# Splitting the feed-forward's first weights during the last tile of the O projection

## The chip, the cores and the metric

The kernel runs on one core of one Trainium2 chip. TensorE (PE) does the matmuls, VectorE (DVE) and ScalarE (ACT) the element-wise work, GpSimd (POOL) some of it and some DMA issues, SyncE (SP) issues most DMAs. The metric is the device time of one execution in microseconds (us); the median of three runs counts.

## The reference

One layer of an encoder block on a sequence of 1024 tokens with 1024 channels, all in fp32:

```python
h = rmsnorm(x, g_mix_pre) * (1 + scale_m) + shift_m
z = h @ w_in                       # attention, pooling, convolution, gates
merged = gate0 * (br_a @ wa) + gate1 * (br_b @ wb) + gate2 * (br_c @ wc)
y = merged @ w_out                 # the O projection
x = x + gate_m * rmsnorm(y, g_mix_post)
h2 = rmsnorm(x, g_ff_pre) * (1 + scale_f) + shift_f
y2 = square(relu(h2 @ w_ff1)) @ w_ff2      # 1024 -> 4096 -> 1024
return x + gate_f * rmsnorm(y2, g_ff_post)
```

## The kernel before, in words

Every matmul operand is kept as two parts of a reduced fp32 format, hi and lo. A split is two instructions: ACT copies the value into the reduced format (hi, L693), and DVE subtracts that copy from the value (lo, L694). A product then is three matmuls for each 128 rows of the contraction: hi by hi, hi by lo, lo by hi.

The part that the change touches lies in the middle of the program, between the merge of the branches and the feed-forward.

**The O projection.** `out_tile(t)` makes one tile of 128 tokens, t = 0 to 7. For each half n of the 1024 output columns it runs 8 steps of k with 3 matmuls each (L1030 to L1032), 48 in all. Its inputs are the merged branches, eight tiles `mg`, split tile by tile into `mh` and `ml` (L997, L998); tile t+1 is split within tile t. When a half is done, ACT squares it with a running sum (L1033). When both are, comes a short chain over ACT and DVE: the reciprocal root of the sum (L232 on ACT, L233 to L239 on DVE), the normalisation, which reads the two PSUM banks (L1040), the sum with x (L1042), its squares (L1044), a second reciprocal root, and the normalised tile `yt` (L1046). The even tiles use the PSUM banks `mm`, the odd ones the two banks `s`.

**The transposes.** `h2T_pair(tp)` transposes the tiles 2tp and 2tp+1 on PE (L1055; four groups of four, in the banks `pt` and `pu`), and ACT and DVE make the feed-forward's operands of them (L1061, L1065, L1068, L1069): `B11`, `B21` from the pairs 0 and 1, `B12`, `B22` from the pairs 2 and 3. The pairs 0 and 1 stand in the program ahead of the tiles 3 and 5, pair 2 behind tile 7, pair 3 behind the first product of the feed-forward. Of the first two pairs, the values also go to DRAM (`h_d`), to be read back later (`hr`, L1183).

**The feed-forward's start.** It is a fast form of block multiplication: for each of 16 column tiles j of the first weights, `first_two(j)` makes two products of 12 matmuls each (`product`, L725 to L727), into a bank X with B11 and into the one bank Y with B21; `last_five(j)` makes five more. The first products of j = 0 to 4 (`EARLY = 5`) are made in a row; meanwhile the sums T1 to T4 of the operands are formed (L734) and split, and the sums of the weights too: `prep_s21(0)` (L704, L705) needs two weight tiles, loaded again by L699, `prep_s34(0)` (L712, L713) as well. `last_five(0)` takes all of these.

**Order.** The tile framework orders the instructions of each engine when the program is built, by their place in the program and by its own estimate of when each can run; the engines then work through their queues in that order. A pool's tiles reuse addresses of a closed pool, and no instruction on a new pool's tile stands ahead of the instructions of the pool that it replaces. `opool` holds the O projection's tiles; when it closes, `fpool` opens in its place, and the PSUM pool `fps` replaces `psum`. The operands `op` of the feed-forward are in `fpool`. `mpool`, the general pool, stays open: its tag `M` has eight buffers of 128x1024 fp32 (4 KB a partition). The eight `mg` tiles fill them; when tile 7 has been split, they are handed on: to `yt` of the tiles 6 and 7, to the weight tiles `w1r` of j = 0 to 4, and to `hr`. The names and lines below are those of the kernel before.

Of the kernel before, what the change touches and what calls it, by code (L numbers as in the profile page):

```python
# [9 lines left out]
F32R = mybir.dt.float32r  # L10
BF16 = mybir.dt.bfloat16
AF = mybir.ActivationFunctionType
# [5 lines left out]
KT = D // P  # L18
# [3 lines left out]
HALF = 512  # L22
# [31 lines left out]
def kernel(  # L54
# [18 lines left out]
    V, A, G, T = nc.vector, nc.scalar, nc.gpsimd, nc.tensor  # L73
# [5 lines left out]
    def open_pool(name, **kw):  # L79
        guards[name] = tc.tile_pool(name=name, bufs=1, reuse_waits="tile", **kw)  # L80
        return guards[name].__enter__()
# [4 lines left out]
    mpool = open_pool("mpool")  # L86
# [16 lines left out]
    def ps(tag, shape=(P, HALF)):  # L103
        if tag == "pt" and two[0]:
            two[1] ^= 1
            tag = ("pt", "pu")[two[1]]
        uid[0] += 1
        return psum.tile(list(shape), F32, tag=tag, name=f"ps_{tag}_{uid[0]}", bufs=PBUFS[tag])

    def f32(ap):  # L110
        return ap.bitcast(F32)
# [76 lines left out]
    for n in range(2):  # L188
        pcb = ps("pt")
        for i in range(4):  # L190
            k = 4 * n + i
# [35 lines left out]
    def rstd(ssq, r):  # L227


        n = ssq.shape[-1]  # L230
        u, w, q = (small.tile([P, n], F32, tag=f"r{i}", name="ru") for i in range(3))
        A.activation(u, ssq, AF.Sqrt, bias=epst, scale=0.25 / D)  # L232
        V.tensor_scalar(w, ssq, 0.25 / D, 0.25 * EPS, op0=ALU.mult, op1=ALU.add)  # L233
        V.reciprocal(q, u)
        for i in range(n):
            cs = slice(i, i + 1)
            V.scalar_tensor_tensor(out=w[:, cs], in0=w[:, cs], scalar=q[:, cs], in1=u[:, cs],
                                   op0=ALU.mult, op1=ALU.add)
        return V.reciprocal(r, w)  # L239
# [417 lines left out]
    for hd in range(NH):  # L657
        p = hd // 2
# [26 lines left out]
    def tile_of(pool, tag, bufs, shape=(P, D), dtype=F32, name=None):  # L685
        uid[0] += 1
        return pool.tile(list(shape), dtype, tag=tag, name=f"{name or tag}_{uid[0]}", bufs=bufs)
# [4 lines left out]
    def fsplit(hi, lo, src):  # L692
        i = A.activation(hi, src, AF.Copy)  # L693
        V.tensor_tensor(out=lo, in0=src, in1=f32(hi), op=ALU.subtract)  # L694
        return i

    def load_half(src):
        r = tile_of(mpool, "M", 8, name="w1r")
        nc.sync.dma_start(r, src)  # L699
        return r  # L700
# [19 lines left out]
    def product(p, o, c0, bs, start):  # L720
        for k in range(4):
            ks = slice(c0 + k * P, c0 + (k + 1) * P)
            a, b = o[:, 0, ks], o[:, 1, ks]
            r0, r1 = bs[k]
            T.matmul(p, a, r0, start=(start and k == 0), stop=False, skip_group_check=True)  # L725
            T.matmul(p, a, r1, start=False, stop=False, skip_group_check=True)  # L726
            i = T.matmul(p, b, r0, start=False, stop=(k == 3), skip_group_check=True)  # L727
        return i

    def two_parts(t):  # L730
        return t[:, 0, :], t[:, 1, :]
# [87 lines left out]
    def gate_pair(b, j, r1, o, first, hook):  # L819
# [5 lines left out]
        more_ada(n_ada)  # L825
        X = ps("mm")
        product(X, o, 0, q11, True)
        p1 = snap_of(g_sn(), X)
        Y = ps("av")
# [129 lines left out]
    for j in range(KT):  # L959
# [6 lines left out]
        for n, b in enumerate((1, 2, 0)):  # L966
            for hf in range(2):
                cs = slice(hf * HALF, (hf + 1) * HALF)
                pp = gemm_T(wts, br, KB[b], hf, BT[b][hf])
                o = m if b == 1 else tmp  # L970
# [20 lines left out]
    def split_mg(t):  # L991

        tk = slice(t * P, (t + 1) * P)
        mh = tile_of(opool, f"mh{t % 2}", 1, (P, KT, P), F32R)
        ml = tile_of(opool, f"ml{t % 2}", 1, (P, KT, P), F32R)
        for k in range(KT):
            A.activation(mh[:, k, :], mg[k][:, tk], AF.Copy)  # L997
            V.tensor_tensor(out=ml[:, k, :], in0=mg[k][:, tk], in1=f32(mh[:, k, :]), op=ALU.subtract)  # L998
        return mh, ml
# [5 lines left out]
    ssy = tile_of(opool, "ssy", 1, (P, NT, 2))  # L1005
# [7 lines left out]
    B12 = [tile_of(h2pool, "b12", 4, (P, HALF)) for _ in range(4)]  # L1013
    B22 = [tile_of(h2pool, "b22", 4, HT, F32R) for _ in range(4)]

    def out_tile(t):

        xt = tile_of(opool, "x2", 2)
        nc.sync.dma_start(xt, x[t])
        mh, ml = mhl.pop(0)  # L1020
        if t < NT - 1:
            mhl.append(split_mg(t + 1))
        pss = []

        yt = tile_of(opool, "yt", 4) if t < 6 else tile_of(mpool, "M", 8, name="yt")
        for n in range(2):
            p = ps("mm" if t % 2 == 0 else "s")
            ns = slice(n * HALF, (n + 1) * HALF)
            for k in range(KT):
                T.matmul(p, mh[:, k, :], wo[k][0][:, ns], start=(k == 0), stop=False)  # L1030
                T.matmul(p, mh[:, k, :], wo[k][1][:, ns], start=False, stop=False)
                T.matmul(p, ml[:, k, :], wo[k][0][:, ns], start=False, stop=(k == KT - 1))  # L1032
            A.activation(yt[:, ns], p, AF.Square, accum_out=ssy[:, t, n:n + 1])  # L1033
            pss.append(p)
        V.tensor_tensor(out=ssy1[:, t:t + 1], in0=ssy[:, t, 0:1], in1=ssy[:, t, 1:2], op=ALU.add)
        rstd(ssy1[:, t:t + 1], rsy[:, t:t + 1])
        for n in range(2):
            ns = slice(n * HALF, (n + 1) * HALF)
            y = yt[:, ns]
            V.scalar_tensor_tensor(out=y, in0=pss[n], scalar=rsy[:, t:t + 1], in1=gmb[:, ns],  # L1040
                                   op0=ALU.mult, op1=ALU.mult)
            V.tensor_tensor(out=xt[:, ns], in0=xt[:, ns], in1=y, op=ALU.add)  # L1042
        nc.gpsimd.dma_start(x2_d[t], xt)
        A.activation(yt, xt, AF.Square, accum_out=ss2[:, t:t + 1])  # L1044
        rstd(ss2[:, t:t + 1], rs2[:, t:t + 1])
        V.tensor_scalar(yt, xt, rs2[:, t:t + 1], None, op0=ALU.mult)  # L1046
        return yt

    def h2T_pair(tp, xs, bank, h_tile):
        for k0 in range(0, KT, 2):  # L1050
            p = bank()
            for kk in range(2):
                for i in range(2):
                    o = kk * 256 + i * P
                    T.transpose(p[:, o:o + P], xs[i][:, (k0 + kk) * P:(k0 + kk + 1) * P], ident)  # L1055
            for kk in range(2):
                k = k0 + kk
                cs = slice((tp % 2) * 256, (tp % 2 + 1) * 256)
                src = p[:, kk * 256:(kk + 1) * 256]
                if tp >= 2 and k < 4:  # L1060
                    A.activation(B12[k][:, cs], src, AF.Identity, bias=modc[:, 24 + k:25 + k], scale=af[:, k:k + 1])  # L1061
                    continue
                b = B11[k] if k < 4 else (B22 if tp >= 2 else B21)[k - 4]
                h = h_tile()[:, 0:256]
                A.activation(h, src, AF.Identity, bias=modc[:, 24 + k:25 + k], scale=af[:, k:k + 1])  # L1065
                if tp < 2:
                    nc.gpsimd.dma_start(h_d[k // 2][:, k % 2, cs], h)
                A.activation(b[:, 0, cs], h, AF.Copy)  # L1068
                V.tensor_tensor(out=b[:, 1, cs], in0=h, in1=f32(b[:, 0, cs]), op=ALU.subtract)  # L1069

    h2t = lambda: tile_of(opool, "h2t", 3, (P, 256))
    pairs = []
    for tp in range(4):
        x0 = out_tile(2 * tp)
        if 0 < tp < 3:
            h2T_pair(tp - 1, pairs[tp - 1], lambda: ps("pt"), h2t)
        pairs.append((x0, out_tile(2 * tp + 1)))
    h2T_pair(2, pairs[2], lambda: ps("pt"), h2t)

    close_pool("opool")  # L1080
    close_pool("wopool")
# [5 lines left out]
    def fbank(tag, bufs):  # L1087
        return tile_of(fps, tag, bufs, (P, HALF))
# [6 lines left out]
    def prep_a(j):  # L1095
        r = load_half(w_ff1[j])
        o = f_op()
        fsplit(o[:, 0, :], o[:, 1, :], r)
        return r, o
# [17 lines left out]
    def snap(p):  # L1117
        s_ = tile_of(fpool, "sn", 3, (P, HALF))
        A.activation(s_, p, AF.Copy)
        return s_  # L1120

    def plus(p, s_):
        V.tensor_tensor(out=s_, in0=p, in1=s_, op=ALU.add)
        return s_
# [1 line left out]
    prod_i = [None]  # L1126

    def first_two(j):
        r1, o = prep_a(j)
        X = fbank("X", 5)  # L1130
        product(X, o, 0, [two_parts(t) for t in B11], True)
        s1 = snap(X)
        Y = fbank("Y", 1)
        prod_i[0] = product(Y, o, HALF, [two_parts(t) for t in B21], True)
        c = plus(Y, s1)
        if j < EARLY:

            r = tile_of(fpool, "ur", 3, (P, HALF))
            A.activation(c, c, AF.Relu)
            A.activation(r, c, AF.Square)  # L1140
            nc.gpsimd.dma_start(u_d[0][j // 2][:, j % 2, :], r)
        else:
            relu2(0, j, c)
        return X, r1
# [220 lines left out]
    for t in range(NT):  # L1365
# [5 lines left out]
        for n, y in order:  # L1371
            ns = slice(n * HALF, (n + 1) * HALF)
# [6 lines left out]
        for n, _ in order:  # L1379
            ns = slice(n * HALF, (n + 1) * HALF)  # L1380
# [71 lines left out]
```

## Time and profile before

| | us |
|---|---|
| median of three runs | 1443.53 (1442.56 to 1444.18) |
| the profiled execution's own time | 1444.37 |
| its span in the profile | 1442.5 |
| PE busy | 1395.1 (97% of the span) |
| DVE busy | 1011.9 (70%) |
| ACT busy | 630.1 (44%) |

Times in the profile are counted from the start of the span. "Busy" is the time in which an engine executes instructions. A row of a timeline gives start, duration, engine, line, operation, what is written and read, its shape and how many alike follow each other; in brackets stands how long the engine was idle before it, and what it then waited for. The O projection runs from 713.9 to 806.9 us, the feed-forward's first products start at 815.25 us.

### The profile page before, as it was taken

To read this page: it belongs to the slowest core of one execution; us is meant where nothing else is said; L and a number is where in the kernel's file an instruction comes from. 1 tells how busy PE (TensorE), PEld (TensorE's weight loads), DVE (VectorE), ACT (ScalarE), POOL (GpSimd) and SP (SyncE) were. 2 spreads that over 40 slices of the span, in tenths; PEclk is the share of its full clock that TensorE was granted. 3 is DMA by queue.
4 is the path that set the end of the run, shared out by engine and by line. 5 is a ranking of instruction groups with operands and counts; after the bars stand their busy time and mean duration, and the time that the engine had idled before them with its cause. 6 is when DMAs were issued, how large, how long until landed. Compare 5 with 4: busy or idle time off the path is not lost.

```text
span 1442.5 us, 18454 instructions
## 1 busy us (share of the span) xinstructions
PE 1395.1 (97%) x6599; PEld 1149.4 (80%) x6599; DVE 1011.9 (70%) x1907; ACT 630.1 (44%) x1112; POOL 202.9 (14%) x313
## 2 busy tenths in 40 slices
PE   6999999999999999999999899999999999999997
PEld 5998888887877777778788678888888788888875
DVE  7653589796979866378756698555553448997587
ACT  6712466456844433342155563333332343434353
POOL 1002334333311101100012011111111000000230
PEclk9999999999999999999999999999999999999999
DMA  8411111202136765377523534333322886535333
GB/s 307 178 45 46 58 30 60 89 30 85 55 102 223 260 213 190 128 271 258 187 92 128 212 117 161 117 117 110 110 88 89 340 292 204 163 101 189 104 110 138
DMA packets 64853, 209.02 MB, mean 145 GB/s; under 512 B 8873, under 2 KB 9977, under 8 KB 64762
## 3 DMA queue, kind: packets, MB, share of 16 engines
q1 hardware_dynamic: 53818, 172.18, 36.1%
q0 software_dynamic: 10944, 35.67, 6.5%
q8 instruction: 52, 0.85, 0.2%
q14 instruction: 39, 0.32, 0.1%
HBM read 163.73 MB, written 44.09 MB: 144 GB/s over the span
## 4 chain that ended last, share of the span: by engine, by line
PE 72%; DVE 12%; DMA 8%; issue 5%; ACT 2%; POOL 0%; SPq 0%; DVEq 0%; ACTq 0%; POOLq 0%
PE ps_mm L347 4%; PE ps_mm L346 4%; PE ps_mm L345 4%; PE X L1251 4%; PE X L727 4%; PE X L1250 4%; PE X L1252 4%; PE X L726 4%; PE X L725 3%; DMA wa<-in_w_ada_dram 3%; PE Y L1251 3%; PE Y L1250 3%; PE Y L1252 3%; PE ps_av L536 2%; PE Z L727 2%
## 5 line engine op out<-in xcount | busy, mean ns | idle before, releaser
L693 ACT ACTIVATE uh<-u 128x1024 fp32r<-128x1024 f32 x56 | 59.5, 1062 | 160.3 <-PE X L1251 70.3
L694 DVE TENSOR_TENSOR ul<-u,uh 128x1024 fp32r<-128x1024 f32 x56 | 69.4, 1238 | 75.9 <-ACT uh L693 75.9
L345 PE MATMUL ps_mm<-hT,whi 128*128 128x512 f32 x272 | 107.7, 396 | 0.4 <-DVE kl L451 0.4
L347 PE MATMUL ps_mm<-hT,wlo 128*128 128x512 f32 x272 | 107.5, 395 | 0.0
L346 PE MATMUL ps_mm<-hT,whi 128*128 128x512 f32 x272 | 107.2, 394 | 0.0
L1251 PE MATMUL X<-wl,uh 128*128 128x512 f32 x256 | 100.1, 391 | 1.4 <-DVE wl L694 1.4
L694 DVE TENSOR_TENSOR op<-s,op 128x1024 fp32r<-128x1024 f32 x52 | 63.6, 1223 | 53.9 <-ACT op L693 53.9
L1250 PE MATMUL X<-wh,uh 128*128 128x512 f32 x256 | 99.5, 390 | 0.7 <-ACT sn L1296 0.7
L1252 PE MATMUL X<-wh,ul 128*128 128x512 f32 x256 | 99.7, 389 | 0.0
L224 DVE CUSTOM_DVE_ANT_0 wa<-wa,cb,colt 128x1024 f32<-128x1024 f32 x48 | 61.1, 1282 | 25.9 <-DMA wa<-in_w_ada_dram 25.9
L1251 PE MATMUL Y<-wl,uh 128*128 128x512 f32 x192 | 75.1, 391 | 0.0
L1252 PE MATMUL Y<-wh,ul 128*128 128x512 f32 x192 | 74.8, 389 | 0.0
L693 ACT ACTIVATE op<-s 128x1024 fp32r<-128x1024 f32 x52 | 54.8, 1057 | 42.1 <-PE Y L727 21.2
L1250 PE MATMUL Y<-wh,uh 128*128 128x512 f32 x192 | 72.1, 389 | 0.0
L694 DVE TENSOR_TENSOR wl<-w2r,wh 128x1024 fp32r<-128x1024 f32 x56 | 69.5, 1241 | 0.2 <-ACT wh L693 0.2
L1115 POOL DMA_DIRECT2D u_d<-ur x58 | 31.4, 542 | 242.5 <-DVE ur L1114 242.5
L509 POOL TENSOR_SCALAR prob<-prob,sm 128x128 f32<-128x128 f32 (+3 forms) x64 | 51.7, 808 | 90.4 <-DVE sm L508 83.9
L536 PE MATMUL ps_av<-PT,vS 128*128 128x256 f32 x320 | 60.3, 295 | 2.3 <-ACT PT L114 1.2
L693 ACT ACTIVATE wh<-w2r 128x1024 fp32r<-128x1024 f32 x56 | 58.8, 1051 | 7.1 <-DVE w2r L1351 1.8
L536 PEld LDWEIGHTS ps_av<-PT,vS 128*128 128x128 f32 x320 | 48.1, 188 | 15.3 <-ACT PT L114 6.9
L1376 POOL TENSOR_TENSOR yl<-sn,gfb 128x512 f32<-128x512 f32 x12 | 24.3, 2032 | 252.5 <-DVE ul L694 236.4
L345 PEld LDWEIGHTS ps_mm<-hT,whi 128*128 128x128 f32 x272 | 51.1, 188 | 9.6 <-POOL kh L450 0.6
(440 smaller groups left out, 4015.5 us busy)
## 6 DMA issues: line engine op xcount, KB each, us to landing
w2r<-in_w_ff_dram SPq DMA_DIRECT2D x64, 512.0 KB, 3.9
wa<-in_w_ada_dram SPq DMA_DIRECT2D x48, 512.0 KB, 5.1
w1r<-in_w_ff_dram SPq DMA_DIRECT2D x37, 512.0 KB, 3.9
u<-u_d SPq DMA_DIRECT2D x32, 512.0 KB, 5.2
u_d<-ur POOLq DMA_DIRECT2D x63, 256.0 KB, 2.3
sig_d<-sig POOLq DMA_DIRECT2D x48, 256.0 KB, 3.5
sig<-sig_d SPq DMA_DIRECT2D x48, 256.0 KB, 4.2
wr<-in_w_in_dram SPq DMA_DIRECT2D x20, 512.0 KB, 3.7
```

The costliest lines, as they stand in the source:

```text
L224: V.tensor_tensor_reduce(out=w, in0=w, in1=cbs[0], scale=1.0, scalar=colt[:, C_BADA + i:C_BADA + i + 1], op0=ALU.mult, op1=ALU.add, accum_ ...
L345: T.matmul(p, a, r0, start=(i == 0), stop=False)
L346: T.matmul(p, a, r1, start=False, stop=False)
L347: T.matmul(p, b, r0, start=False, stop=(i == n - 1))
L536: last_pe[0] = T.matmul(av[:, :256], st, PT[:, pp, offs[jj]:offs[jj] + 256], start=(j == 0 and pp == 0), stop=(j == nj - 1 and pp == 1))
L693: i = A.activation(hi, src, AF.Copy)
L694: V.tensor_tensor(out=lo, in0=src, in1=f32(hi), op=ALU.subtract)
L726: T.matmul(p, a, r1, start=False, stop=False, skip_group_check=True)
L727: i = T.matmul(p, b, r0, start=False, stop=(k == 3), skip_group_check=True)
L1250: T.matmul(bank[t], a, r0, start=(first and k == 0), stop=False, skip_group_check=True)
L1251: T.matmul(bank[t], a, r1, start=False, stop=False, skip_group_check=True)
L1252: T.matmul(bank[t], b, r0, start=False, stop=(last and k == 1), skip_group_check=True)
```

## The change

Four things are done. The operand of column tile 0 of the feed-forward's first weights is loaded and split ahead of `out_tile(7)`, and its hi and lo parts lie in two buffers of the general pool (`M`) instead of one `op` tile of `fpool`. `h2T_pair(2)` moves from behind tile 7 to ahead of it. The square of tile 7's second half is placed behind the new split in ACT's queue (`issue_after`). And in tile 0 of the O projection the last step of k of the first half is taken behind the whole second half; the two PSUM banks of a tile are asked for together.

```diff
     def product(p, o, c0, bs, start):
         for k in range(4):
             ks = slice(c0 + k * P, c0 + (k + 1) * P)
-            a, b = o[:, 0, ks], o[:, 1, ks]
+            a, b = (o[0][:, ks], o[1][:, ks]) if isinstance(o, list) else (o[:, 0, ks], o[:, 1, ks])
...
+    o_i = None
+
     def out_tile(t):
...
         pss = []
 
         yt = tile_of(opool, "yt", 4) if t < 6 else tile_of(mpool, "M", 8, name="yt")
-        for n in range(2):
-            p = ps("mm" if t % 2 == 0 else "s")
-            ns = slice(n * HALF, (n + 1) * HALF)
-            for k in range(KT):
+        pss = [ps("mm" if t % 2 == 0 else "s") for _ in range(2)]
+
+        for n, ks in ((0, range(KT - 1)), (1, range(KT)), (0, (KT - 1,))) if t == 0 else ((0, range(KT)), (1, range(KT))):
+            p, ns = pss[n], slice(n * HALF, (n + 1) * HALF)
+            for k in ks:
                 T.matmul(p, mh[:, k, :], wo[k][0][:, ns], start=(k == 0), stop=False)
                 T.matmul(p, mh[:, k, :], wo[k][1][:, ns], start=False, stop=False)
                 T.matmul(p, ml[:, k, :], wo[k][0][:, ns], start=False, stop=(k == KT - 1))
-            A.activation(yt[:, ns], p, AF.Square, accum_out=ssy[:, t, n:n + 1])
-            pss.append(p)
+            if k == KT - 1 and n == 1 and o_i is not None:
+                with tc.issue_after(o_i.ins):
+                    A.activation(yt[:, ns], p, AF.Square, accum_out=ssy[:, t, n:n + 1])
+            elif k == KT - 1:
+                A.activation(yt[:, ns], p, AF.Square, accum_out=ssy[:, t, n:n + 1])
...
     for tp in range(4):
         x0 = out_tile(2 * tp)
-        if 0 < tp < 3:
+        if tp:
             h2T_pair(tp - 1, pairs[tp - 1], lambda: ps("pt"), h2t)
+        if tp == 3:
+
+            r1_0 = load_half(w_ff1[0])
+            o_0 = [tile_of(mpool, "M", 8, dtype=F32R, name=n) for n in ("oh", "ol")]
+            o_i = fsplit(o_0[0], o_0[1], r1_0)
         pairs.append((x0, out_tile(2 * tp + 1)))
-    h2T_pair(2, pairs[2], lambda: ps("pt"), h2t)
...
     def first_two(j):
-        r1, o = prep_a(j)
+        r1, o = prep_a(j) if j else (r1_0, o_0)
```

## Rows read from the trace of the kernel before

**Rows 1.** The page, part 1: busy us, share of the span, instructions.
```profile
PE 1395.1 (97%) x6599; PEld 1149.4 (80%) x6599; DVE 1011.9 (70%) x1907; ACT 630.1 (44%) x1112; POOL 202.9 (14%) x313
```
**Rows 2.** Timeline of PE, from the O projection's tile 5 on.
```profile
772.06 0.60 PE L1055 MATMUL ps_pt<-ident,yt 128*128 128x128 f32 x4
...
784.98 0.39 PE L1030 MATMUL ps_mm<-woh,mh 128*128 128x512 f32 x1
...
795.86 0.39 PE L1030 MATMUL ps_s<-woh,mh 128*128 128x512 f32 x1
...
806.86 0.60 PE L1055 MATMUL ps_pt<-ident,yt 128*128 128x128 f32 x4
...
815.25 0.80 PE L725 MATMUL X<-b,op 128*128 128x512 f32 x1 [4.79 <-ACT op L693]
...
822.73 1.04 PE L1055 MATMUL X<-ident,yt 128*128 128x128 f32 x8
...
860.59 0.50 PE L725 MATMUL X<-t,op 128*128 128x512 f32 x1 [0.29 <-ACT op L693]
```
**Rows 3.** Windows: length; busy us (instructions) of PE, PEld, DVE, ACT, POOL; clock; DMA.
```profile
816.00:820.00 4.00, 3.96 (x12) 2.81 (x11) 3.87 (x4) 2.05 (x3) 0.00 (x0) 0.64 0.66 163
820.00:850.00 30.00, 30.00 (x142) 25.09 (x141) 26.35 (x44) 22.52 (x43) 2.18 (x4) 1.00 0.34 119
850.00:870.00 20.00, 19.64 (x85) 15.33 (x84) 19.79 (x29) 10.48 (x15) 2.17 (x4) 1.00 0.61 206
```
**Rows 4.** Timeline of ACT around the end of the O projection.
```profile
801.66 0.58 ACT L1033 ACTIVATE yt<-ps_s 128x512 f32<-128x512 f32 x1
...
807.06 0.60 ACT L1033 ACTIVATE yt<-ps_s 128x512 f32<-128x512 f32 x1 [4.55 <-PE ps_s L1032]
...
814.16 3.89 ACT L693 ACTIVATE op<-w1r 128x1024 fp32r<-128x1024 f32 x4
```
**Rows 5.** Timeline of DVE, from the normalised tile 6 to the weight sums.
```profile
803.20 0.75 DVE L1046 TENSOR_SCALAR yt<-x,rs 128x1024 f32<-128x1024 f32 x1
...
814.19 0.75 DVE L1046 TENSOR_SCALAR yt<-x,rs 128x1024 f32<-128x1024 f32 x1
...
815.23 4.63 DVE L694 TENSOR_TENSOR op<-w1r,op 128x1024 fp32r<-128x1024 f32 x4
823.00 0.69 DVE L1123 TENSOR_TENSOR sn<-Y,sn 128x512 f32<-128x512 f32 x1 [3.13 <-PE Y L727]
...
825.77 0.69 DVE L704 TENSOR_TENSOR s<-w1r 128x512 f32<-128x512 f32 x1
...
828.84 0.69 DVE L705 TENSOR_TENSOR s<-s,w1r 128x512 f32<-128x512 f32 x1
...
850.99 1.23 DVE L694 TENSOR_TENSOR op<-s,op 128x1024 fp32r<-128x1024 f32 x1
```
**Rows 6.** Waits of PE between 700 and 1150 us: total, times, longest.
```profile
PE ps_mm L1032 <- DVE ml L998: 1.3, 1, 1.3
```
**Rows 7.** Timeline of SP's DMA queue.
```profile
793.98 2.49 SPq L699 DMA_DIRECT2D w1r<-in_w_ff_dram  x5
796.57 22.51 SPq L1183 DMA_DIRECT2D hr<-h_d  x4
...
816.49 2.59 SPq L1183 DMA_DIRECT2D hr<-h_d  x3
819.89 5.00 SPq L699 DMA_DIRECT2D w1r<-in_w_ff_dram  x2
```
**Rows 8.** DMA issues in windows from 816, 818, 819.3 and 824.5 us: us to landing.
```profile
hr<-h_d SPq DMA_DIRECT2D x1, 512.0 KB, 3.4
...
hr<-h_d SPq DMA_DIRECT2D x1, 512.0 KB, 5.3
...
w1r<-in_w_ff_dram SPq DMA_DIRECT2D x1, 512.0 KB, 5.4
...
w1r<-in_w_ff_dram SPq DMA_DIRECT2D x1, 512.0 KB, 3.5
```

## The prediction

> **What bounds the kernel now.** Begin with the page's first part: PE is busy for 97% of the span [rows 1], so only a place where PE stands still, or does less than it could, can give much. The view of waits and the timeline of PE show such a place at the end of the O projection: tile 7 ends at 806.86, where the transposes of pair 2 begin, and the first product of the feed-forward starts at 815.25, after an idle of 4.79 us that ended with ACT's split of the first weights [rows 2]. That is 8.39 us for four groups of transposes. PE then runs for some microseconds at a granted clock of 0.64 on average, between its levels of 1.2 and 2.4 GHz [rows 3]: at 2.4 GHz those 4 us would have been about 1.4 us shorter.
>
> Next, who is busy behind the place. In the windows from 820 to 850 and 850 to 870 us DVE works 26.35 of 30 and 19.79 of 20 us [rows 3], and at 860.59 PE waits for an operand that ACT and DVE make [rows 2]. The reader is to see two engines that arrive together: PE starts late, and DVE is only just in time. An earlier PE is worth only what DVE can follow.
>
> The timeline of DVE gives its chain: the normalised tile 7 (L1046) at 814.19, the lo parts of four weight tiles from 815.23, 3.13 us of idle until the product Y, then without a longer pause the sums and splits up to the operand of `prep_s34(0)`, which starts at 850.99 and takes 1.23, so that it ends at about 852.2 [rows 5].
>
> **The first split.** It leaves the place where it holds PE: ACT's share of the four at 814.16 is 3.89/4 = 1.0 us [rows 4], DVE's 4.63/4 = 1.16 us [rows 5]. They go to where ACT idles 4.55 us at a time [rows 4]; DVE has like pauses in a tile's chain. If that cover were gone, they would cost their 1.0 and 1.16 us. The load goes to SP's queue ahead of tile 7's x; the buffer it needs is free once tile 7's `mg` is split, within tile 6 (784.98 to 795.86 [rows 2]). I take no cost, and 0 to 1 us as bounds.
>
> **Pair 2.** Its sixteen transposes now stand in tile 7. What that costs is read from tile 5, which carries pair 1: 784.98 − 772.06 = 12.92 us, against 806.86 − 795.86 = 11.00 for tile 7 without a pair [rows 2], so 1.92 us. Tile 7 ends at 808.8. Pair 2 issues no DMA, and no queue but PE's, ACT's and DVE's is changed by its move.
>
> **What PE gains.** The first product can start at 808.8 and, with Y behind it, is done by about 815. The transposes of pair 3 come next, and these need the normalised tile 7. In tile 6 that took from PE's end at 795.86 to 803.20 + 0.75 = 803.95 [rows 5], 8.1 us, of which some 0.5 went to a square of the next tile (0.58 us at 801.66) that stood ahead on ACT [rows 4]; tile 7 has no such follower. So 808.8 + 7.6 = 816.4, against 822.73 before [rows 2]: PE gains 6.3 us here, with waits of some 1.5 us left. The other splits, of j = 1 to 4, still lie in `fpool`, so they still stand behind everything of the O projection: before, the weights were issued from 793.98 on [rows 7], ACT was idle until 807.06, and its splits came at 814.16 all the same [rows 4].
>
> **What DVE gains.** Its lo parts start behind tile 7's L1046, at 816.4 instead of 815.23: 1.2 us later, because of pair 2. It has one split of 1.16 us less to do, and loses its 3.13 us of idle, as Y is done long before. The end at 852.2 moves by 1.2 − 1.16 − 3.13 = −3.1 us, at most −3.7 with the smaller pauses. DVE's 3.1 is the bound, not PE's 6.3; the rest becomes waiting of PE for banks and operands.
>
> **The general pool.** This is the step that decides. Before, the eight buffers held `yt` twice, five `w1r`, and one `hr`, which was issued at 796.57, long before its use [rows 7]. Now `yt` twice, the first weights, their hi and lo, and three `w1r` fill them; the fourth `w1r` takes over the first weights' buffer. So the first `hr` has no buffer until a lo part in the new era is done, at 816.4 + 1.16 = 817.6. Six loads of 512 KB now follow each other there (four `hr`, and the two weight tiles of `prep_s21(0)`, call them r2 and r1), where five did. SP issues in order, so r2 and r1 are behind all the `hr`.
>
> Their landings: before, the first of the stacked loads was issued at 816.49 and took 3.4 us, until 819.9; the fourth, r2, was issued at 819.89 and took 5.4, until 825.3 [rows 7, 8]. That is 5.4 us for three further loads, 1.8 each; the last step, from the third load (818.75 + 5.3 = 824.1) to the fourth, is 1.2. Now the first lands at 817.6 + 3.4 = 821.0, r2, the fifth, at 825.8 to 828.2, and r1, the sixth, at 827.0 to 830.0. L705, which needs r1, ran at 828.84, 0.4 us after r1's landing at 824.89 + 3.5 = 828.4 (its issue is the last of the two, 819.89 + 5.00 [rows 7, 8]). DVE would come there 3.1 us earlier, at 825.7. It stands 1.3 to 4.3 us, in the middle 2.8; the steps of 1.8 and 1.2 are equally near, so I take the middle. The queue keeps its order, so only work that happens to stand ahead of L704 and L705 fills the stall; from none to all of it, I take 0.2 us.
>
> The Trainium skill, page DMA: Bandwidth & Descriptors, section Anatomy of one DMA — SWDGE (gpsimd) path, gives about 2.0 us and the bytes at 436 GB/s for a transfer, a fit for another issue path. As an estimate by that page, 524 KB take 3.2 us, so r1 would land at about 824.4, before DVE comes to it, and the sum would be that of the second case below. The trace agrees for a load that runs alone (3.4 and 3.5 us) and not for stacked ones (5.3 and 5.4) [rows 8].
>
> **Tile 0.** Three matmuls move from the end of the first half to the end of the second; none is added. PE's wait there is 1.3 us for an `ml` [rows 6], at the first step of k, which keeps its place. So 0; a gain could not exceed 1.3. The first half's square (0.6 us) now comes at the tile's end; tile 0 is next needed by pair 0, two tiles of 11 us later, which hide it.
>
> **The sum.** −3.1 + 2.8 − 0.2 = −0.5 us, from the profiled execution's 1444.37 to 1443.9. The median of the runs shown is 0.84 lower, so the time is 1443.0. A change under 0.2% (2.9 us, 1440.6 to 1446.4) cannot be told from none here.
>
> **The cases.**
>
> - *The stall moves* (chance 0.46), as summed: the seam closes, DVE waits for r2 and r1. By the bounds of the landings, −1.8 to +1.2 us: 1441.7 to 1444.7.
> - *DVE alone is the bound* (0.20): DVE's queue has enough other work ahead of L704 and L705, or the loads land as a lone one does. −3.1 to −3.7 us, 1440.4 to 1439.8. For it: some 23 us of DVE's work lie between L705 and 852.2. Against it: the sums for T2 are ready late too, as they hang on the same transposes.
> - *PE's gain stays whole* (0.09): the queues come out so that nothing that PE needs before 870 us is late: −6.3 us, 1437.2. Against it stand the 19.79 of 20 us of DVE [rows 3].
> - *Slower* (0.15): L704 keeps its place as one of the first instructions behind the weights' splits. Before, it ran at 825.77, 0.5 us after r2's landing; now DVE would be there at 822.7 and stand until r2 lands, at the late end 828.2, 2.4 us later than before. Everything behind it in the queue is late by that, the reading of the one Y bank too; PE, idle for over 4 us there as it was at 815, then runs at the lower clock again, 1.4 us more: 1447.3. It decides from a landing of r2 after 825.8 on, in that place.
> - *The split gets in its own way* (0.10): ACT or DVE stands for its load within tile 6 or 7, pair 2 is late, tile 7 too. Up to 1 us for each us of standing, and at 3.1 nothing is left of the gain: about 1443.5.
>
> The Trainium skill, page Perfetto Trace Analysis, section Identifying the Most-Contended Engine, says to optimise the engine with the highest occupancy; by that the idle time of PE is worth its length, which is the third case. The same page, section Optimization Strategy, says that the most-contended engine can change over a kernel; the windows bear that out here.
>
> **How the numbers follow.** The likeliest case gives 1443.0. The range reaches down to 1439.8, the end of the second case, and up to 1446.0, short of the fourth; outside lie the third and most of the fourth, about 2 in 10. The second case lies about two thirds beyond the bound of 0.2%: faster 0.09 + 0.15 = 0.24. Slower is most of the fourth, 0.15. The rest, 0.61, is no change.
>
> **What would show it.** In the profile after: tile 7 takes about 12.9 us and ends near 808.8; the first product follows it with no wait for ACT, at 2.4 GHz; the transposes of pair 3 start near 816.4; the first `hr` is issued near 817.6 and not at 797; DVE shows idle time that ends with a landing of r2 or r1; PE waits in the products of j = 1 to 4 or at the start of `last_five(0)`. Were DVE busy without such a wait from 816 to 849, the second case holds. The prediction is wrong if `hr` finds a buffer early, if the splits of j = 1 to 4 run before tile 7's chain ends, or if r1 lands after 830.

## The result and the profile after

The changed kernel took 1451.79 us in the median of four runs (1449.53 to 1453.22), the kernel before in the same session 1443.05; the ratio is 1.0063, with a 95% interval of 1.0052 to 1.0075. It is slower by nearly 9 us, and outside the range on record (1439.8 to 1446.0).

The profiled execution of the changed kernel was 3.68 us ahead when tile 6 began (781.30 against 784.98 us [rows 2]), and the O projection up to there took 71.04 us in both traces (from 710.26 and from 713.94): the lead comes from the stages ahead of it, which the change leaves alone, and is called drift below. So times are compared from there: from the first matmul of tile 6 to the last of `last_five(1)` the kernel before needs 89.45 us (to 874.43) and the changed one 98.14 (to 879.44): 8.69 more. Behind it the two differ by 0.14. The loss lies in this stretch, and the page's first part, here of the changed kernel, hides it: against [rows 1] DVE and ACT do the same work, and PE is busy for 3.6 us longer.

```profile
PE 1398.7 (97%) x6599; PEld 1152.8 (80%) x6599; DVE 1011.2 (70%) x1907; ACT 629.9 (44%) x1112; POOL 202.4 (14%) x313
```

The timeline of PE after the change, which answers to [rows 2] (lines of the changed kernel stand 3 to 10 further down: L1032 is now L1035, L1040 L1046, L1046 L1052, L1055 L1061, L1065 L1071, L1068 L1074, L1114 L1124, L1119 L1129, L1183 L1193):

```profile
781.30 0.40 PE L1033 MATMUL ps_mm<-woh,mh 128*128 128x512 f32 x1
...
805.27 0.39 PE L725 MATMUL X<-b,oh 128*128 128x512 f32 x1
...
808.83 0.50 PE L725 MATMUL Y<-b,oh 128*128 128x512 f32 x1 [0.60 <-DVE yt L1046]
...
811.74 0.28 PE L1061 MATMUL X<-ident,yt 128*128 128x128 f32 x1
812.98 0.98 PE L1061 MATMUL X<-ident,yt 128*128 128x128 f32 x7 [0.97 <-DVE yt L1052]
...
826.18 0.80 PE L725 MATMUL X<-b,op 128*128 128x512 f32 x1 [5.05 <-ACT op L693]
...
852.07 0.50 PE L725 MATMUL X<-t,op 128*128 128x512 f32 x1 [1.94 <-ACT op L693]
...
864.37 0.80 PE L725 MATMUL X<-t,op 128*128 128x512 f32 x1 [3.16 <-ACT op L693]
...
879.44 0.39 PE L727 MATMUL X<-t,oc 128*128 128x512 f32 x1
```

The seam is closed, as forecast: the first product follows tile 7 with no wait, and the transposes of pair 3 begin at 811.74. With the drift taken off, before's began at 819.05 (822.73 − 3.68 [rows 2]), so PE is 7.3 us ahead. Only the first transpose, which needs tile 6 alone, runs then; the others wait for the normalised tile 7 until 812.98, and are 6.1 us ahead. Then it loses all of it and more: it stands 5.05 us before the product of j = 2, 1.94 before T3's product and 3.16 before `last_five(1)`. The windows, against [rows 3], and two shorter ones around the first of these waits:

```profile
816.00:820.00 4.00, 4.00 (x18) 3.27 (x18) 2.99 (x6) 3.37 (x8) 0.54 (x1) 1.00 0.77 238
820.00:850.00 30.00, 24.95 (x101) 19.94 (x100) 23.33 (x36) 18.84 (x33) 2.17 (x4) 0.89 0.24 83
850.00:870.00 20.00, 14.76 (x55) 11.08 (x55) 19.84 (x30) 9.24 (x14) 1.62 (x3) 0.91 0.54 194
...
820.00:826.00 6.00, 1.13 (x5) 0.59 (x4) 1.09 (x3) 2.44 (x5) 0.00 (x0) 0.78 0.35 139
826.00:830.00 4.00, 3.82 (x9) 3.08 (x10) 4.00 (x5) 4.00 (x7) 0.55 (x1) 0.50 0.36 101
```

From 820 to 826 us all three engines stand nearly still (1.13, 1.09 and 2.44 of 6 us), so none of them is the bound; and from 826 to 830 PE has its lower level of clock, 0.50. DVE, which the prediction had as the bound, worked 23.33 of 30 us where it had 26.35, and has that work still to do.

Who is waited for is read from the timeline of ACT:

```profile
813.44 1.06 ACT L693 ACTIVATE op<-w1r 128x1024 fp32r<-128x1024 f32 x1 [1.47 <-DVE yt L1052]
...
817.24 1.03 ACT L1071 ACTIVATE ur<-Z,modc,af 128x256 f32<-128x256 f32 x2
818.14 0.74 ACT L1074 ACTIVATE b<-ur 128x256 fp32r<-128x256 f32 x2
818.76 0.61 ACT L1129 ACTIVATE sn<-X 128x512 f32<-128x512 f32 x1
823.56 1.02 ACT L1071 ACTIVATE ur<-Z,modc,af 128x256 f32<-128x256 f32 x2 [4.19 <-DMA u_d<-ur]
824.47 0.71 ACT L1074 ACTIVATE b<-ur 128x256 fp32r<-128x256 f32 x2
825.09 1.99 ACT L693 ACTIVATE op<-w1r 128x1024 fp32r<-128x1024 f32 x2
```

Two things meet here. One split (j = 1) stands at 813.44 where four stood in a row before [rows 4]; those of j = 2 and 3 come at 825.09, behind all of pair 3's work. And within pair 3's work ACT stands 4.19 us for a buffer: pair 3 writes its values into `ur`, a ring of three buffers, which also takes the feed-forward's results on their way to DRAM (`u_d`). The first product's result has one of the three, so the third of pair 3's values finds no buffer until the first write of `u_d` has landed. DVE waits with it, then runs to the operand of `prep_s34(0)`:

```profile
815.67 1.95 DVE L734 TENSOR_TENSOR b<-b,hr 128x512 f32<-128x512 f32 x3
...
824.91 0.76 DVE L1075 TENSOR_TENSOR b<-ur,b 128x256 fp32r<-128x256 f32 x2 [4.95 <-ACT b L1074]
...
838.52 0.68 DVE L704 TENSOR_TENSOR s<-w1r 128x512 f32<-128x512 f32 x1
...
852.05 1.22 DVE L694 TENSOR_TENSOR op<-s,op 128x1024 fp32r<-128x1024 f32 x1
```

That operand is 1.06 us later than before by the clock (852.05 against 850.99 [rows 5]) and 4.7 with the drift taken off. The write is issued at 816.74, behind five of the six loads (the four `hr` and r2; r1 follows only at 827.43), which SP's queue and the landings in windows from 815.5 and 816 us (microseconds to landing at the end) show:

```profile
811.69 4.41 SPq L1193 DMA_DIRECT2D hr<-h_d  x4
816.15 0.42 SPq L699 DMA_DIRECT2D w1r<-in_w_ff_dram  x1
...
hr<-h_d SPq DMA_DIRECT2D x1, 512.0 KB, 5.9
w1r<-in_w_ff_dram SPq DMA_DIRECT2D x1, 512.0 KB, 7.5
u_d<-ur POOLq DMA_DIRECT2D x1, 256.0 KB, 6.8
```

In the kernel before the same write was issued at 825.78, when the `hr` and r2 had landed and one load was under way. Its landing, and ACT's wait for it:

```profile
u_d<-ur POOLq DMA_DIRECT2D x1, 256.0 KB, 3.2
...
829.06 1.02 ACT L1065 ACTIVATE ur<-Z,modc,af 128x256 f32<-128x256 f32 x2 [0.68 <-DMA u_d<-ur]
```

Laid along the stretch, by the same matmuls in both traces and with the drift taken off: 8.26 us ahead at the end of the first product into X; 2.97 of it go around pair 3's transposes, 5.22 by the start of j = 2 (the wait of 5.05), 2.01 in the lower clock behind that, 2.12 and 0.44 around T3 (the wait of 1.94), 2.96 before `last_five(1)` (the wait of 3.16) and 1.23 in the lower clock after it: −8.26 + 16.95 = 8.69, as measured.

### The profile page after: what moved, and what is told of

Its sections match the earlier page's. It is cut to its first block, busy times and chain, and to the rows that moved or that the text cites. A ratio compares the mean times of both kernels' runs of the same rounds, so it can differ in the third digit from the quotient of the medians.

```text
span 1447.7 us, 18454 instructions
## 1 busy us (share of the span) xinstructions
PE 1398.7 (97%) x6599; PEld 1152.8 (80%) x6599; DVE 1011.2 (70%) x1907; ACT 629.9 (44%) x1112; POOL 202.4 (14%) x313
## 4 chain that ended last, share of the span: by engine, by line
PE 79%; DVE 9%; issue 4%; DMA 4%; ACT 2%; POOL 0%; DVEq 0%; SPq 0%; ACTq 0%; POOLq 0%
PE ps_mm L347 5%; PE ps_mm L346 5%; PE ps_mm L345 5%; PE X L725 4%; PE X L726 4%; PE X L727 4%; PE X L1261 4%; PE X L1260 4%; PE X L1262 4%; PE Y L1261 3%; PE Y L1260 3%; PE Y L1262 3%; PE ps_av L536 2%; DMA wa<-in_w_ada_dram 2%; PE Z L725 2%
```

## The experiments

The theories: **A**, the wait for a `ur` buffer makes the loss; **B**, the order does, as three splits stand behind pair 3's work on ACT; **C**, the stacked loads of the prediction. The column "stretch" is the profiled execution's own, from tile 6 to the end of `last_five(1)`, against before's 89.45 us; it can differ from the medians by up to 3 us, since single executions do (the stages ahead of tile 6 alone came out between 4.6 us sooner and 0.4 later than in before's).

| kernel | median us | ratio (95%) | stretch |
|---|---|---|---|
| the change | 1451.79 | 1.0063 (1.0052 to 1.0075) | +8.7 |
| e1: pair 3's temporaries in t4's ring | 1454.64 | 1.0077 (1.0056 to 1.0099) | +2.9 |
| e2: splits ahead of pair 3 | 1447.58 | 1.0035 (1.0019 to 1.0052) | +5.5 |
| e3: e1 and e2 | 1453.17 | 1.0069 (1.0048 to 1.0090) | +2.4 |
| e4: tile 0 as before | 1452.54 | 1.0062 (1.0039 to 1.0084) | +10.2 |
| e5: temporaries in t1's ring | 1444.80 | 1.0024 (1.0010 to 1.0039) | +2.6 |
| e6: e5 and e2 | 1442.64 | 1.0002 (0.9991 to 1.0014) | +3.0 |
| e7: early split alone | 1444.40 | 1.0016 (1.0005 to 1.0027) | +2.2 |
| e8: pair 2 in tile 7 alone | 1444.87 | 1.0015 (1.0004 to 1.0027) | +2.0 |
| e9: hr behind the first u_d | 1447.83 | 1.0039 (1.0026 to 1.0052) | +6.4 |
| e10: tile 0's order alone | 1442.02 | 0.9997 (0.9988 to 1.0007) | +0.4 |
| e11: e6, prep_s21(1) earlier | 1440.06 | 0.9981 (0.9969 to 0.9993) | −2.3 |
| e12: e11, T4's sums on POOL | 1443.21 | 1.0003 (0.9994 to 1.0013) | +1.8 |
| e13: before, prep_s21(1) earlier | 1441.62 | 0.9991 (0.9982 to 1.0000) | +0.4 |
| e14: e7 with e5's ring | 1441.11 | 0.9993 (0.9983 to 1.0003) | −0.2 |
| e15: e14, prep_s21(1) earlier | 1441.01 | 0.9985 (0.9975 to 0.9995) | −1.0 |

**Own temporaries (e1).** Pair 3 no longer shares `ur`:

```diff
-        h2T_pair(3, pairs[3], t_bank, lambda: tile_of(fpool, "ur", 3, (P, HALF)))
+        h2T_pair(3, pairs[3], t_bank, lambda: tile_of(tpool, "t4", 4, (P, 256)))
```

> The changed kernel, with one edit: the f32 temporaries of pair 3's transposes come from a ring of their own in the small pool (four of 128x256) and no longer from the three ur buffers that the products' sums share; the order of the queues should stay. Theory A (the wait for a ur buffer): in the changed kernel ACT stands 4.19 us at 823.56 for the write u_d<-ur, which took 6.8 us to land, and the splits of j = 2 to 4 stand behind it. Without that wait, ACT's splits come some 4 us earlier, PE's wait of 5.05 us before the product of j = 2 is at most about 1 us, the lower clock behind it is gone, and the time is about 5 + 1.8 us below the changed kernel's: 1443 to 1446. Theory B (the order alone: the splits of j = 2 to 4 stand behind pair 3's work on ACT, whatever that work waits for): the wait of ACT moves to another cause, PE still waits 3 us or more before the product of j = 2, and the time stays within 2 us of the changed kernel's 1451.8. Theory C (the stacked loads of hr, r2 and r1 of the prediction): no effect on the time, 1450 to 1453.

The stretch did as A says (5.8 us came back), the time did not. The view of waits from 1100 to 1150 us of this kernel shows why:

```profile
PE X L1260 <- ACT sn L1306: 7.0, 1, 7.0
```

A stall 300 us later, of which the changed kernel has only 0.7 us: 8.25 us lost behind the stretch. SP's load of the second weights waited there for `PE X L727`, a product. The likely cause, which no trace shows directly: asking for t4 first placed it at the start of its pool, where the second weights' first buffer lies later, so that their load waits for the last product to read T4. The experiment had its own fault, and e5 takes it out.

**Splits first (e2), and both (e3).** The loads and splits of j = 1 to 4 are written ahead of pair 3:

```diff
+    preps = {0: (r1_0, o_0)}
     begun = [first_two(0)]
+    preps.update((j, prep_a(j)) for j in range(1, EARLY))
...
-        r1, o = prep_a(j) if j else (r1_0, o_0)
+        r1, o = preps.pop(j, None) or prep_a(j)
```

> The changed kernel, with the loads and splits of j = 1 to 4 written ahead of pair 3's transposes, so that ACT and DVE find them there first; the ur buffers are as in the changed kernel. Theory A (the wait for a ur buffer): ACT still stands about 4 us for u_d<-ur, now with the splits ahead of it, so PE's product of j = 2 starts on time, but pair 3's B22 and B12 and the snaps behind them are late by what is left of the wait: about half the loss, 1445 to 1449. Theory B (the order alone): the 5.05 us of PE and the lower clock behind it are gone, and the time is 1442 to 1445. Theory C (stacked loads): no effect, 1450 to 1453.

> The changed kernel with both edits: own temporaries for pair 3, and the splits of j = 1 to 4 ahead of it. Theory A and theory B agree that nothing is left of the stall, so this tells what the change itself is worth: DVE's chain to the operand of prep_s34(0) starts some 3 us earlier than before and PE has 6 to 7 us in hand, 1437 to 1441, if nothing else is late next. Theory C (stacked loads of hr, r2, r1): 1447 to 1453, as in the changed kernel.

e2 gives half of the loss back, as A had it; ACT still stood 2.8 us for `u_d`. e3 has e1's fault (6.8 us at the same place), so its time says nothing on its forecast; its stretch, 2.4 us longer than before's, already speaks against it.

**Tile 0 (e4, e10).** The order of tile 0 taken back, and tile 0's order as the only edit to the kernel before:

```diff
-        for n, ks in ((0, range(KT - 1)), (1, range(KT)), (0, (KT - 1,))) if t == 0 else ((0, range(KT)), (1, range(KT))):
+        for n, ks in ((0, range(KT)), (1, range(KT))):
```

> The changed kernel with tile 0 in its old order (the last k of the first half directly behind the others). All theories of the stall at the seam: no difference from the changed kernel, 1450 to 1453, since tile 0 ends some 60 us ahead of the seam. If the new order of tile 0 has a part in the loss, the time is below 1449, and PE's offset at tile 1 shows it.

> The kernel before with tile 0's new order alone. The prediction's step: three matmuls change places, nothing is added, the wait for ml stays at the first k, so no difference: 1441 to 1444. If the tile's order matters, tile 0's time from its first to its last matmul differs by more than 0.3 us.

Both as expected: tile 0 has no part in it.

**The fault taken out (e5, e6).** As e1 and e3, with `"t1"`, the ring that came first anyway, in place of `"t4"`.

> The changed kernel with pair 3's temporaries in a ring of their own, as in the first run of this kind, but in t1's ring, which was the first of the small pool before too. In the first run they were in t4's, which put t4 at the start of the pool, where the second feed-forward's first weights are loaded later: PE stood 7.0 us for those at 1126 us. Theory A (the wait for a ur buffer makes most of the loss at the seam, and the 7 us at 1126 came from the place of t4): in the stretch from 790 to 870 us PE loses about 3.4 us against the kernel before, as in the first run, where the changed kernel loses 9.3; there is no stall at 1126; 1445.5 to 1447.5. Theory B (own temporaries put pair 3 where it holds up what comes later, whatever the place of t4): the stall at 1126 stays and the time is 1451 to 1455.

> The same with the splits of j = 1 to 4 written ahead of pair 3. Theory A: 2.9 us lost from 790 to 870 us, of which the lower clock behind PE's waits of about 2 us at 848 and 860 is most, and no stall at 1126; 1445 to 1447, so even without the wait for ur the change gains nothing, as VectorE is the bound behind the seam. If the gain of PE at the seam stays whole, 1437.

The stall at 1126 is gone (0.7 us, as before). Without the wait for `ur` most of the loss is gone: 7.0 us by the medians (1451.79 to 1444.80), 6.1 in the stretch. PE's waits in e5 show which of the changed kernel's three belonged to it:

```profile
822.97 0.50 PE L725 MATMUL X<-b,op 128*128 128x512 f32 x1 [0.75 <-ACT op L693]
...
846.99 0.50 PE L725 MATMUL X<-t,op 128*128 128x512 f32 x1 [1.94 <-ACT op L693]
...
859.32 0.50 PE L725 MATMUL X<-t,op 128*128 128x512 f32 x1 [3.16 <-ACT op L693]
```

The wait of 5.05 before j = 2 is 0.75; those of 1.94 and 3.16 stand as they were, so they are not its doing. The order is worth 2.2 us on top of that by the medians (e6), though the two stretches are alike (+2.6 and +3.0); with `ur` as it was (e2), 4.2. A and B are both right. C, by which such edits change nothing, is not, though its stacked loads come back below as what makes the write slow. With both mended, nothing is gained over the kernel before (e6's ratio is 1.0002; its forecast, 1445 to 1447, was too slow). e6's waits of PE from 786 to 880 us say where the gain went:

```profile
PE X L725 <- ACT op L693: 4.3, 2, 2.2
```

One of 2.11 us before T3's product (845.71) and one of 2.21 before `last_five(1)` (858.23). DVE is the bound ahead of the first: it worked 29.59 of the 30 us from 816 to 846. At 853.34 DVE itself stood for PE, and then did L1124 twice before the sums that `last_five(1)` needs; in the kernel before the sums stood in between these (L704 at 856.94, L705 at 858.74).

**The parts alone (e7, e8).** e7 has the early split, e8 only `h2T_pair(2)` within tile 7.

```diff
-        if tp:
+        if 0 < tp < 3:
             h2T_pair(tp - 1, pairs[tp - 1], lambda: ps("pt"), h2t)
...
+    h2T_pair(2, pairs[2], lambda: ps("pt"), h2t)
```

> The early split in the general pool alone: pair 2 behind tile 7 and tile 0 as before. Theory A (the wait for ur and the place of the splits come from the early split, as the first product is queued ahead of the other splits): ACT stands for u_d<-ur and the splits of j = 2 to 4 stand behind pair 3 here too; PE gains less at the seam (pair 2 still lies there), so PE comes out later than in the changed kernel: 1450 to 1454. Rival (the loss comes from pair 2 and tile 7, or needs both parts): 1441 to 1445.

> Pair 2 within tile 7 alone: the first weights are split in fpool as before, and tile 0 is as before. Theory A: the splits of j = 0 to 3 stand ahead of pair 3 on ACT as before, the seam loses the pair's work behind tile 7 but the splits still wait for tile 7's chain; first product near 815 as before, less 1 us at most: 1441 to 1444. Rival (the loss comes from pair 2's place): above 1446.

Neither makes the loss: each costs some 2 us, and the two together nearly 9. For e7 the rival was right, not A (1450 to 1454); e8 fell between its two forecasts. e8's price is plain: the splits still wait for tile 7's chain, tile 7 ends later by pair 2's work, and PE stands 7.05 us instead of 4.79 [rows 2]. e7 has the wait for `ur` (3.29 us), but all four splits stand ahead of pair 3; so the early split alone doesn't put pair 3 first. It also shows the wait that the prediction had bet on, for r2's landing:

```profile
824.67 0.69 DVE L704 TENSOR_TENSOR s<-w1r 128x512 f32<-128x512 f32 x1 [2.12 <-DMA w1r<-in_w_ff_dram]
```

**Why the write is slow (e9).** The changed kernel, with the loads of `hr` issued behind the first write of `u_d`, on POOL's queue instead of SP's:

```diff
-        nc.sync.dma_start(r, h_d[i])
+        with tc.issue_after(u_i[0]):
+            nc.gpsimd.dma_start(r, h_d[i])
```

> The changed kernel with the four loads of hr issued behind the first write u_d<-ur, on that write's queue, and no longer ahead of it on SP's. Theory A1 (the write takes 6.8 us because the hr loads, issued from 5 us before to 1 us before it, share the DMA engines with it): the first write of u_d lands in about 3 us, ACT's wait for a ur buffer shrinks from 4.19 to 1 us or less, and the seam loses 3 to 5 us less than in the changed kernel, if hr, some 6 us later, holds nothing up: 1444 to 1449. Theory A2 (the write is slow for another reason): it still takes 5 us or more and the time is 1450 to 1454.

The write landed in 3.1 us, ACT's wait for it was gone, and the time fell by 4 us in the median (2.3 in the stretch, where 3 to 5 were forecast):

```profile
u_d<-ur POOLq DMA_DIRECT2D x1, 256.0 KB, 3.1
```

So A1 holds: a write on POOL's queue lands late behind loads issued before it on SP's. In the changed kernel it landed 0.1 us before r2, the load issued last ahead of it; the four `hr` loads that e9 issues behind it did not hold it up. The Trainium skill, page DMA: Bandwidth & Descriptors, section Issuing engines are not separate DMA queues, says that transfers from different engines run on the same 16 DMA engines and interleave. The traces agree (6.8 against 3.1 us). That DVE's work slowed it is not borne out: in the kernel before, DVE worked from 825.16 to 829.4 without a break while the write took 3.2 us, and in the changed kernel DVE had stood idle for 3.6 us when the write landed. The rest of e5's gain is missing in e9: DVE could begin `hr`'s subtractions only at 825.46 us instead of 815.67, and PE still stood 3.16 us before T3's product and 3.36 before `last_five(1)`.

**VectorE's order and load (e11, e12).** e6 with the sums for j = 1 written ahead of `last_five(0)`, and then also T4's four subtractions on POOL:

```diff
         if j == 0:
+            *rs_1, o21_1 = prep_s21(1, None)
             last_five(j, begun[j][0], None, o21_0, o34_0, o4_0)
+        elif j == 1:
+            last_five(j, begun[j][0], None, o21_1, *prep_s34(*rs_1))
...
-        tsum(r, r, t2s[k], ALU.subtract)
+        nc.gpsimd.tensor_tensor(out=r, in0=r, in1=t2s[k], op=ALU.subtract)
```

> The changed kernel with pair 3's temporaries in t1's ring, the splits of j = 1 to 4 ahead of pair 3, and the loads, sums and split of prep_s21(1) written ahead of last_five(0). In the run without this last edit PE waits 2.2 us before last_five(1) at 858 and runs at the lower clock behind it (1.7 us), as VectorE takes the sums of prep_s21(1) only behind the squares of last_five(0); in the kernel before they stood between those. Theory D (VectorE's queue order makes that wait): the second wait and its clock loss go, 3 to 4 us less than that run: 1438.5 to 1440.5. Rival (VectorE's amount of work or the weights' landing makes it): the wait stays or moves to o34 of j = 1; 1441.5 to 1444.

> The same, with the four subtractions for T4 done by GpSimd, which is nearly idle there; one takes some 2 us there by the kernel's own 128x512 products, against 0.6 on VectorE. Theory D (VectorE is the bound from the seam to the first last_five): 2.4 us of its work go, PE's wait before T3 at 846 (2.1 us, and 1.3 of clock) shrinks and the time is 1 to 3 us below the run without it: 1436 to 1440. Rival (T4 on the slower engine is late, or the wait is one of order): no gain or a loss, 1439 to 1443.

e11 is the first that beats the kernel before, by 0.19% (0.07 to 0.31): the wait before `last_five(1)` is gone, that of 2.11 before T3 stays. Its profiled execution lost 1.6 of the stretch's 2.3 us again behind it, around a wait of 1.05 us at 1282 for which no cause was sought. e12 brought no gain, as its rival had it (1443.21, just above the rival's range). The timelines of POOL and then of DVE in e12:

```profile
827.07 4.04 POOL L1218 TENSOR_TENSOR hr<-hr,t2s 128x512 f32<-128x512 f32 x1 [7.06 <-DVE t2s L734]
...
831.66 2.55 POOL L1218 TENSOR_TENSOR hr<-hr,t2s 128x512 f32<-128x512 f32 x2
...
836.67 1.65 POOL L1218 TENSOR_TENSOR hr<-hr,t2s 128x512 f32<-128x512 f32 x1 [1.94 <-DVE t2s L734]
```

```profile
830.46 4.31 DVE L694 TENSOR_TENSOR t<-t2s,t 128x512 fp32r<-128x512 f32 x2
```

A subtraction on POOL took 1.3 to 4.04 us, and while POOL worked, two of DVE's that take 1.28 together took 4.31. DVE lost what it was to gain, and PE's wait before T3 grew to 3.88 us.

**What the gain belongs to (e13 to e15).** e13 is the kernel before with e11's first lines alone, e14 the early split with pair 3's temporaries in t1's ring, e15 both.

> The kernel before with the one edit that made the best version so far faster: prep_s21(1) written ahead of last_five(0). If that version's gain is the seam's (the change with its two faults mended), this edit alone brings nothing here, since PE waits only 0.29 us before last_five(1): 1441 to 1444. If the gain is the edit's own, 1439.5 to 1440.5.

> The early split alone (pair 2 behind tile 7, tile 0 as before), with pair 3's temporaries in t1's ring. Without them this kernel's ACT stood 3.3 us for a ur buffer, and PE then 4.83 us before the Y product of j = 2 with the lower clock behind it. Theory A (that wait is what the early split costs, with no part in it of pair 2): about 5 us of the stretch come back, of which VectorE's bound behind the seam keeps some 2: 1439 to 1442. Rival (the loads: VectorE's wait of 2.1 us for r2's landing is in the way all the same): 1442 to 1445.

> The same with prep_s21(1) ahead of last_five(0). If VectorE's order before last_five(1) is late here too, 1 to 3 us less than the run without it: 1438 to 1441; if not, the same time.

That the reordered sums bring a part of e11's gain by themselves is not shown: e13's time is what its expectation gave for no effect, its ratio is lower by 0.09% with an interval that reaches 1, and its stretch is 0.4 us longer than before's. e14 is faster than e7 by 3.3 us in the median and 2.4 in the stretch, which is what `ur` costs the early split alone; the wait for r2 (2.45 us) stays in it. e15 is clear of the kernel before (0.9985), not of e14. Between e11, e14 and e15 these runs can't choose: their intervals overlap.

## Why the prediction was wrong

**The step that failed** is the sentence that the other splits "still stand behind everything of the O projection", with the conclusion that an earlier PE only meets DVE. It is true of the O projection, and it was read as if their place behind nothing else mattered. In the changed kernel pair 3's work went ahead of j = 2 to 4 on ACT; that pair 3 was simply ready first, once the first product no longer waited, is argued and not shown. With it came a resource that the prediction left out, and so put at nothing: the three `ur` buffers, and the write that frees them. Instead of DVE, ACT held PE: it stood 4.19 us for the write, PE 5.05 us behind it, and 2.0 more went in the lower clock; without that wait (e5) the stretch is 6.1 us shorter. The view of waits of the kernel before had the line (ACT stood 0.7 us for `u_d<-ur`); it was not among its rows. At 0.7 us it looked like nothing, but the write was to move from a place with one load under way to one behind five, and those loads were in the prediction's own sum. Experiments e5 and e9 settle this.

**A second step failed** once that wait is out of the way: that what DVE gains at the operand of `prep_s34(0)` is what the kernel gains. In e6 DVE is 2.1 us earlier there, and the stretch is still 3.0 us longer than before's. The place behind it was left out: the sums for `last_five(1)` had fallen behind other work in DVE's queue, and PE stood 2.21 us for them. With these sums put earlier (e11) the stretch is 2.3 us shorter than before's, near the 3.1 that the second case gave.

Point by point:

- *First split, 0 us*: right; no engine stands for it in tiles 6 and 7. The square placed behind it in ACT's queue starts when tile 7 ends (805.47), so that part of the change costs nothing either.
- *Pair 2, 1.92 us*: right. Tile 6 and 7 took 23.97 us (781.30 to 805.27) against 21.88 [rows 2]: 2.09 more.
- *PE gains 6.3 us at pair 3, which needs the normalised tile 7*: right. The transposes that need it began 6.1 us earlier (812.98, or 816.66 with the drift put back, where 816.4 was forecast).
- *DVE is the bound behind the seam, 3.1 us gained*: as the place of the bound, right once the two faults are mended; 2.1 us instead of 3.1. In e6 the operand of `prep_s34(0)` is begun at 845.69 against 850.99 [rows 5], with that run 3.16 us ahead at tile 6. The term that was too small is the late start of the lo parts: 3.0 us, not 1.2 (815.05 in e6, or 818.2 with its lead put back, against 815.23), as DVE stood 1.00 us there for ACT's hi part. PE's lead then ends in waits of 2.11 and 2.21 us and the clock behind these. In the changed kernel itself the operand is 4.7 us later.
- *General pool, first hr at 817.6, a stall of 2.8 us*: wrong for the changed kernel. `hr` found a buffer at 811.69, when the first products had read the weights' hi and lo parts; I had counted only the buffers that a lo part frees. That was a sign of error that the prediction had named, and r1's landing after 830 (831.1) another. Nobody waited for r2, as DVE came to L704 at 838.52. In e7 and e14, where DVE is on time, the wait is there, with 2.12 and 2.45 us. One reading was off, to no effect on the sum: before, r1's issue began at 824.56 and not 824.89, so it landed 0.7 us ahead of L705.
- *Lower clock, 1.4 us, in the slower rival*: about right. The stretch lost 2.0 us behind the wait of 5.05, and 1.2 behind that of 3.16.
- *Tile 0, 0 us*: right (0.9997, 0.9988 to 1.0007).
- *The slower rival* had the right form, an engine standing in its queue with PE idle behind it at the lower clock, and the wrong engine, place and transfer: ACT for a write, not DVE for a load. Its size was one wait of 2.4 us; the changed kernel has three, of 5.05, 1.94 and 3.16, and the last two stand without the write's delay as well (e5). That its sign came true is luck in part.

## What to carry to other kernels

When a step is moved earlier, look at each ring of buffers that its followers share with a transfer, not only at engines and loads: a wait of 0.7 us said here that the ring was at its end, and the price was the transfer's landing time in the new place. If an instruction no longer holds its followers back, ask which of them will be queued first. An operand that is ready sooner gains nothing if the next one that PE needs has fallen back in the same queue. And a change in the order in which rings are asked for can be paid for by a later stage, here with 8 us some 300 us on.

## What the runs showed of the hardware

The first 256 KB write of `u_d` took 3.1 to 3.2 us with at most one load under way ahead of it (before, e8, e9) and 6.3 to 7.5 us behind five or six stacked loads of 512 KB from another queue (the changed kernel, e2, e5, e6, e7, e11). In each of these six it landed 0.1 to 0.4 us before the load that was issued last ahead of it.

DVE and POOL held each other up: a DVE subtraction of 128x512 with both inputs in SBUF, 0.68 us elsewhere, took up to 3.19 us while POOL subtracted, and POOL's own took 4.04 us while DVE went on at its pace, against 1.29 and 1.31 when POOL held DVE up. The Trainium skill, page SBUF — State Buffer, section SBUF: two separate sides, describes a port pair that the two share by an exclusive lock, for DVE instructions with two SBUF inputs among others; these times fit it, and no run here separates the port from another cause.
